# Value products with a head's high and low columns side by side as the stationary operand

## The chip, the cores and the metric

The kernel runs on one core of a Trainium2 chip. The metric is the device time of one execution in microseconds (us), the median of several runs. The core has a matrix engine (TensorE, PE), a vector engine (VectorE, DVE), an activation engine (ScalarE, ACT), a general engine (GpSimd, POOL) and an engine that issues transfers (SyncE, SP). Each works through its own instructions in the order in which they are written; semaphores make one wait for another. Products are summed in PSUM, 2 KB banks that PE writes and ACT and DVE read; everything else on the core lies in SBUF. L581 is line 581 of the kernel.

## The reference, cut to what matters

Two layers of an encoder trunk over 256 positions of width 2048. The change touches the attention; its softmax over three dilated windows comes down, at 256 positions, to one masked softmax for each head.

```python
for l in range(DEPTH):                       # 2
    h = rmsnorm(x, g_pre_mix[l])
    proj = h @ w_in[l]                       # conv | q, k, v of 16 heads x 64 | pooling
    y_a = conformer_conv(...)
    y_b = dilated_attention(proj[..., a_end:b_end], cos, sin)
    y_c = pool_mixer(...)
    y = concatenate([rms_normalize(y_a), rms_normalize(y_b), rms_normalize(y_c)]) * g_mix[l]
    x = x + rmsnorm(y @ w_out[l], g_post_mix[l])
    x = x + rmsnorm(SwiGLU(rmsnorm(x, g_pre_ffn[l])), g_post_ffn[l])
```

In `dilated_attention` each head's output is `o = einsum('bnrhqk,bnkrhe->bnqrhe', p, vwin)` over its 64 value columns, divided by the softmax sum.

## The kernel before

All large products are made in split precision: an operand is kept as a high part (fp32r) and a low part (what is left of the fp32 value), and a product is high x high + high x low + low x high. Weights come in tiles of 128x2x512: SP loads them (raw), ACT writes the high half (L104), DVE the low half (L113), and PE uses them in L139 to L141. Eight such tiles (hl) are in flight. This stream of weight products fills PE all the time; its groups set the steps in which the program is written. The schedule is manual: what is written first stands first on each engine, and the small work of attention is a set of Python generators (tasks) that each write a piece in one step and then give way for one or more steps. So the order of every engine follows from the yields, and no instruction passes another on its engine.

Attention runs in two halves of eight heads (hf 0 and 1), two heads (a pair, pr) after each other. For one head `head_task` writes, in this order: scores on PE (L540, six products, q and k in split form) into the one PSUM buffer sc; mask and row maximum on DVE (L545, two halves, the tile pt); the negated maximum on POOL (L550); exponentials on ACT (L553); normalisation on DVE (L559, L561); four transposes on PE (L568) into a PSUM buffer tr; the high part of the transposed probabilities pT on ACT (L572) and the low part on DVE (L573); the value products on PE (L581) into po. Two heads share one po tile, one PSUM bank, of which there is only one.

The value products have the value columns of both heads of the pair (128 columns) as the stationary operand and 256 columns of pT as the moving one: for each of the two key tiles high v x high pT, high v x low pT, low v x high pT, six in all. Only the half of the output rows that belongs to the head is used (rows 0 to 63 for an even head, 64 to 127 for an odd one). After the odd head ACT writes the high part yB (L597, one instruction for each head's 64 rows, with the gain gT), ACT the squares (L601), and DVE the low part (L603), all reading po; POOL adds the squares up (L608).

The values themselves are made in `v_done`: when a v product of 128 positions by 512 columns is done, ACT writes its high part (L525) and DVE its low part (L526), one instruction each.

The tiles pt, both pT and sq come from one pool, s2, with 6 buffers in rotation: each new tile takes the oldest buffer and must wait for the last reader of what was in it. Other work between these steps: rope on q and k (L486 to L499) and their transposes (L509, L513, L514), the convolution's sums on DVE (L380) and its layer norm (L395 to L412), transposes of the y parts (L206, with ACT L213 and DVE L216, into yTA and yTC), the output of a projection (L679).

Of the kernel before, what the change touches and what calls it, by code (L numbers as in the profile page):

```python
# [7 lines left out]
F32 = mybir.dt.float32  # L8
F32R = mybir.dt.float32r
AF = mybir.ActivationFunctionType  # L10
ALU = mybir.AluOpType
AX = mybir.AxisListType

P = 128
S = 256
NT = S // P
# [6 lines left out]
HD = 64  # L23
ROT = 16
NHH = HALF_B // HD
# [4 lines left out]
NB = 512  # L30
# [11 lines left out]
def hybrid_encoder_kernel(  # L42
# [6 lines left out]
    nc = tc.nc  # L49
# [4 lines left out]
    s4 = ctx.enter_context(tc.tile_pool(name="s4", bufs=23))  # L54
    s2 = ctx.enter_context(tc.tile_pool(name="s2", bufs=6))
# [115 lines left out]
    def tr_free():  # L171

        k = clock["step"]
        if used.get(k):
            return False
        used[k] = True
        return True
# [57 lines left out]
    rs_in = {}  # L235
# [81 lines left out]
    def mixer_jobs(l):  # L317
        st = {}
# [199 lines left out]
        def v_done(hf):  # L518
            def done(t, ps):
                if t == 0:  # L520
                    st["v", hf] = [
                        s4.tile([P, NT, NB], F32R, tag="s4", name="v") for _ in range(2)
                    ]
                hi, lo = (a[:, t] for a in st["v", hf])
                nc.scalar.activation(hi, ps, AF.Copy, scale=rs_in[t])  # L525
                nc.vector.scalar_tensor_tensor(  # L526
                    lo, ps, rs_in[t], hi.bitcast(F32), ALU.mult, ALU.subtract
                )
            return done

        def head_task(hf, h):
            qT, kT, v = st["qT", hf], st["kT", hf], st["v", hf]
            pr, r0 = h // 2, (h % 2) * HD
            sc = scp.tile([P, NT, S], F32, tag="sc", name="sc")
            pt = s2.tile([P, NT, S], F32, tag="s2", name="pt")
            mx = sm.tile([P, NT], F32, tag="mx", name="mx")
            den = sm.tile([P, NT], F32, tag="den", name="den")
            for t in range(NT):
                for i, (a, b) in enumerate(((0, 0), (0, 1), (1, 0))):
                    nc.tensor.matmul(  # L540
                        sc[:, t], qT[a][r0 : r0 + HD, pr, t * P : (t + 1) * P],
                        kT[b][r0 : r0 + HD, pr], start=i == 0, stop=i == 2,
                    )
            for t in range(NT):
                nc.vector.tensor_tensor_reduce(  # L545
                    pt[:, t], sc[:, t], mask[:, (1 - t) * P : (1 - t) * P + S], 1.0, -3.0e38, ALU.add, ALU.max,
                    accum_out=mx[:, t : t + 1],
                )
            nmx = sm.tile([P, NT], F32, tag="nmx", name="nmx")
            nc.gpsimd.tensor_scalar(nmx, mx, -(HD ** -0.5), None, ALU.mult)  # L550
            yield
            for t in range(NT):
                nc.scalar.activation(  # L553
                    pt[:, t], pt[:, t], AF.Exp, bias=nmx[:, t : t + 1], scale=HD ** -0.5,
                    accum_out=den[:, t : t + 1],
                )
            yield
            rden = sm.tile([P, NT], F32, tag="rden", name="rden")
            nc.vector.reciprocal(rden, den)  # L559
            for t in range(NT):  # L560
                nc.vector.tensor_scalar(pt[:, t], pt[:, t], rden[:, t : t + 1], None, ALU.mult)  # L561
            yield 2
            while not tr_free():
                yield
            pst = trp.tile([P, NT, S], F32, tag="tr", name="tr")
            for kt in range(NT):
                for t in range(NT):
                    nc.tensor.transpose(  # L568
                        pst[:, kt, t * P : (t + 1) * P], pt[:, t, kt * P : (kt + 1) * P], ident
                    )  # L570
            pT = [s2.tile([P, NT, S], F32R, tag="s2", name="pT") for _ in range(2)]
            nc.scalar.activation(pT[0], pst, AF.Copy)  # L572
            nc.vector.tensor_tensor(pT[1], pst, pT[0].bitcast(F32), ALU.subtract)  # L573
            yield 2
            if h % 2 == 0:
                st["po", hf] = pop.tile([P, 2, S], F32, tag="po", name="po")
            po = st["po", hf]
            n = 0
            for kt in range(NT):
                for a, b in ((0, 0), (0, 1), (1, 0)):  # L580
                    nc.tensor.matmul(  # L581
                        po[:, h % 2], v[a][:, kt, pr * P : (pr + 1) * P], pT[b][:, kt],
                        start=n == 0, stop=n == 5,
                    )
                    n += 1
            if h % 2 == 0:
                return
            if pr == 0:
                yB[hf] = [s4.tile([P, 4, S], F32R, tag="s4", name="yB") for _ in range(2)]
            hi, lo = yB[hf]  # L590
            col = G_MX + l * KD + 4 + 4 * hf + pr
            sq = sq_acc
            if (hf, pr) != (0, 0):
                sq = s2.tile([P, S], F32, tag="s2", name="sq")
            rows = [slice(e * HD, (e + 1) * HD) for e in range(2)]
            for e, r in enumerate(rows):
                nc.scalar.activation(  # L597
                    hi[r, pr], po[r, e], AF.Copy, scale=gT[r, col : col + 1]
                )
            for e, r in enumerate(rows):  # L600
                nc.scalar.activation(sq[r], po[r, e], AF.Square)  # L601
            for e, r in enumerate(rows):
                nc.vector.scalar_tensor_tensor(  # L603
                    lo[r, pr], po[r, e], gT[r, col : col + 1], hi[r, pr].bitcast(F32),
                    ALU.mult, ALU.subtract,
                )
            if sq is not sq_acc:
                nc.gpsimd.tensor_tensor(sq_acc, sq_acc, sq, ALU.add)  # L608
            if hf == 1 and pr == 3:
                yield 2  # L610
                ssb = scp.tile([P, NT], F32, tag="sc", name="ssb")
                for t in range(NT):
                    nc.tensor.matmul(
                        ssb[:, t : t + 1], sq_acc[:, t * P : (t + 1) * P], ones,
                        start=True, stop=True,
                    )
                ms = sm.tile([P, NT], F32, tag="msb", name="msb")
                nc.vector.tensor_scalar(ms, ssb, 1.0 / C_B, EPS, ALU.mult, ALU.add)
                rs = sm.tile([P, NT], F32, tag="rsb", name="rsb")
                nc.gpsimd.tensor_tensor(  # L620
                    rs, ms, half_neg.to_broadcast([P, NT]), ALU.pow
                )
                for t in range(NT):
                    rs_b[t] = rs[:, t : t + 1]
# [3 lines left out]
        def attn_task(hf, pace):  # L628
            for h in range(NHH):
                spawn(head_task(hf, h))  # L630
                yield pace[h % len(pace)]
# [126 lines left out]
    for l in range(DEPTH):  # L758
        jobs, load_layer = mixer_jobs(l)
        a = len(groups)  # L760
        add_jobs(jobs)
        seg_info.append((a, len(groups), load_layer, (g_post_mix, l), G_FF + l * KD))
        a = len(groups)
# [31 lines left out]
    for n in range(4):  # L795
        for t in range(NT):
            load_x(t, n)
            g = 2 * n + t
# [4 lines left out]
    gT = cst.tile([P, NG], F32, name="gT")  # L803
# [9 lines left out]
    rows = {}  # L813
# [48 lines left out]
    col = None  # L862
    for si, (g0, g1, load_layer, post, pre) in enumerate(seg_info):
        n = g1 - g0
# [98 lines left out]
        col = pre  # L963
# [55 lines left out]
```

## Time and profile before

| | |
|---|---|
| median of 3 runs | 2235.47 us (2235.39 to 2235.93) |
| profiled execution | 2234.84 us, span 2233.0 us |
| PE busy | 2210.7 us, 99% of the span |
| DVE busy | 1287.8 us, 58% |
| ACT busy | 1056.9 us, 47% |
| POOL busy | 136.4 us, 6% |
| chain that ended last | PE 94%, DVE 3%, ACT 2%, issue 1% |
[...]

Attention of layer 1 lies at about 160 to 310 us of the span. How the views below are read: the table by stretch gives for each stretch the busy time of PE, PE's weight loads (PEld), DVE, ACT and POOL with the number of instructions, then the granted clock, the DMA share and GB/s. The list of waits gives an engine's line, what it waited for, the sum in us, how often, and the longest. The groups give line, engine, operation, output<-inputs, shapes and count, then busy us and mean ns of one, then the idle time before them and what ended it. The timeline gives start, duration, engine, line, what is written from what, and how many in a row (x4); in brackets the engine's idle time just before and what ended it. Ends of PE's products are modelled, so starts are compared.

### The profile page before, as it was taken

To read this page: it belongs to the slowest core of one execution; us is meant where nothing else is said; L and a number is where in the kernel's file an instruction comes from. 1 tells how busy PE (TensorE), PEld (TensorE's weight loads), DVE (VectorE), ACT (ScalarE), POOL (GpSimd) and SP (SyncE) were. 2 spreads that over 40 slices of the span, in tenths; PEclk is the share of its full clock that TensorE was granted. 3 is DMA by queue.
4 is the path that set the end of the run, shared out by engine and by line. 5 is a ranking of instruction groups with operands and counts; after the bars stand their busy time and mean duration, and the time that the engine had idled before them with its cause. 6 is when DMAs were issued, how large, how long until landed. Compare 5 with 4: busy or idle time off the path is not lost.

```text
span 2233.0 us, 26297 instructions
## 1 busy us (share of the span) xinstructions
PE 2210.7 (99%) x9858; PEld 1781.1 (80%) x9858; DVE 1287.8 (58%) x1735; ACT 1056.9 (47%) x1465; POOL 136.4 (6%) x179
## 2 busy tenths in 40 slices
PE   9999999999999999999999999999999999999998
PEld 7888887888888888888778788878888888888886
DVE  5798757445444544445567987565444444444544
ACT  6445756444444443444554566564444444434442
POOL 0001113000000000000210011120000000000002
PEclk9999999999999999999999999999999999999999
DMA  7654355555556555556565544555555555555553
GB/s 264 197 174 137 133 173 171 184 180 187 187 182 187 184 184 187 187 182 199 177 201 177 171 131 150 171 162 187 180 186 186 186 186 180 187 186 183 188 198 122
DMA packets 208608, 400.66 MB, mean 179 GB/s; under 512 B 12730, under 2 KB 16162, under 8 KB 208480
## 3 DMA queue, kind: packets, MB, share of 16 engines
q1 hardware_dynamic: 208448, 398.98, 55.3%
q8 instruction: 77, 1.26, 0.2%
q14 instruction: 51, 0.42, 0.1%
q10 hardware_dynamic: 32, 0.01, 0.0%
HBM read 396.84 MB, written 2.10 MB: 179 GB/s over the span
## 4 chain that ended last, share of the span: by engine, by line
PE 94%; DVE 3%; ACT 2%; issue 1%; DMA 0%; POOL 0%; SPq 0%; DVEq 0%; POOLq 0%; ACTq 0%
PE acc L139 30%; PE acc L140 30%; PE acc L141 30%; PE tr L206 1%; PE sc L540 1%; PE po L581 1%; DVE hl L113 1%; PE tr L568 1%; ACT xT L213 0%; DVE x L290 0%; DVE xT L216 0%; ACT hl L104 0%; ACT junk L200 0%; PE tr L509 0%; PE tr L442 0%
## 5 line engine op out<-in xcount | busy, mean ns | idle before, releaser
L113 DVE TENSOR_TENSOR hl<-raw,hl 128x1024 fp32r<-128x1024 f32 x736 | 905.2, 1231 | 769.3 <-ACT hl L104 767.8
L104 ACT ACTIVATE hl<-raw 128x1024 fp32r<-128x1024 f32 x735 | 776.6, 1059 | 762.7 <-PE acc L141 752.7
L139 PE MATMUL acc<-hl,xT 128*128 128x512 f32 x1984 | 797.0, 402 | 0.0
L140 PE MATMUL acc<-hl,xT 128*128 128x512 f32 x1984 | 787.7, 397 | 0.6 <-DVE hl L113 0.5
L141 PE MATMUL acc<-hl,xT 128*128 128x512 f32 x1984 | 787.4, 397 | 0.0
L141 PEld LDWEIGHTS acc<-hl,xT 128*128 128x128 f32 x1984 | 374.4, 189 | 90.8
L140 PEld LDWEIGHTS acc<-hl,xT 128*128 128x128 f32 x1984 | 374.5, 189 | 88.6 <-DVE hl L113 2.2
L139 PEld LDWEIGHTS acc<-hl,xT 128*128 128x128 f32 x1984 | 374.4, 189 | 88.6
L139 PE MATMUL acc<-hl,fT 128*128 128x512 f32 x704 | 280.1, 398 | 0.0
L141 PE MATMUL acc<-hl,fT 128*128 128x512 f32 x704 | 279.1, 396 | 0.0
L140 PE MATMUL acc<-hl,fT 128*128 128x512 f32 x704 | 279.0, 396 | 0.0
L141 PEld LDWEIGHTS acc<-hl,fT 128*128 128x128 f32 x704 | 132.6, 188 | 32.3
L140 PEld LDWEIGHTS acc<-hl,fT 128*128 128x128 f32 x704 | 132.7, 188 | 31.7
L139 PEld LDWEIGHTS acc<-hl,fT 128*128 128x128 f32 x704 | 132.6, 188 | 31.8
L270 POOL TENSOR_TENSOR out<-out,gain 128x512 f32<-128x512 f32 x20 | 25.8, 1300 | 1448.2 <-ACT junk L200 1448.2
L380 DVE SCALAR_TENSOR_TENSOR cacc<-hT,cwT,cacc 128x241 f32<-128x241 f32 (+14 forms) x240 | 98.7, 469 | 0.0
L208 ACT ACTIVATE fT<-tr 128x512 fp32r<-128x512 f32 x44 | 26.4, 599 | 96.1 <-PE tr L206 96.1
L209 DVE TENSOR_TENSOR fT<-tr,fT 128x512 fp32r<-128x512 f32 x44 | 30.4, 692 | 68.6 <-ACT fT L208 68.6
L200 ACT ACTIVATE junk<-out 128x512 bf16<-128x512 f32 x32 | 20.2, 631 | 68.3 <-DVE out L737 43.4
L707 ACT ACTIVATE sg<-acc,rsin 128x512 f32<-128x512 f32 x44 | 30.4, 691 | 45.6 <-PE acc L141 45.6
L139 PE MATMUL acc<-hl,yB 128*128 128x512 f32 x128 | 51.1, 399 | 0.0
L140 PE MATMUL acc<-hl,yB 128*128 128x512 f32 x128 | 50.7, 396 | 0.0
(150 smaller groups left out, 1299.2 us busy)
## 6 DMA issues: line engine op xcount, KB each, us to landing
raw<-in_w_gate_dram SPq DMA_DIRECT2D x176, 512.0 KB, 3.5
raw<-in_w_up_dram SPq DMA_DIRECT2D x176, 512.0 KB, 3.5
raw<-in_w_down_dram SPq DMA_DIRECT2D x176, 512.0 KB, 3.6
raw<-in_w_in_dram SPq DMA_DIRECT2D x144, 512.0 KB, 3.6
raw<-in_w_out_dram SPq DMA_DIRECT2D x64, 512.0 KB, 3.6
x<-in_x_dram SPq DMA_DIRECT2D x8, 256.0 KB, 6.9
pm<-in_c_pool_dram SPq DMA_DIRECT2D x4, 512.0 KB, 5.2
gain<-in_g_post_mix_dram SPq DMA_DIRECT2D x4, 512.0 KB, 6.6
```

Of the source, the lines that this page charges most:

```text
L104: nc.scalar.activation(hl[:, 0], raw, AF.Copy)
L113: nc.vector.tensor_tensor(hl[:, 1], raw, hl[:, 0].bitcast(F32), ALU.subtract)
L139: nc.tensor.matmul(ps, xh, hl[:, 0, j], start=first, stop=False)
L140: nc.tensor.matmul(ps, xh, hl[:, 1, j], start=False, stop=False)
L141: nc.tensor.matmul(ps, xl, hl[:, 0, j], start=False, stop=last)
L206: nc.tensor.transpose(pst[:, j], srcs[j], ident)
L208: nc.scalar.activation(dst[:, 0], pst, AF.Copy)
L209: nc.vector.tensor_tensor(dst[:, 1], pst, dst[:, 0].bitcast(F32), ALU.subtract)
L270: nc.gpsimd.tensor_tensor(o, o, gain, ALU.mult)
L380: nc.vector.scalar_tensor_tensor(acc[:, c, lo:hi], src, w, acc[:, c, lo:hi], ALU.mult, ALU.add)
L540: nc.tensor.matmul(sc[:, t], qT[a][r0 : r0 + HD, pr, t * P : (t + 1) * P], kT[b][r0 : r0 + HD, pr], start=i == 0, stop=i == 2,)
L707: nc.scalar.activation(sg[t], ps, AF.Silu, scale=rs_in[t])
```

## The change

The value tile of one key tile is now laid out as 8 heads x 2 x 64: an even head's high columns come first and its low columns behind them, an odd head's low columns first. So 128 columns of one head are the stationary operand, and one product gives high v x pT in 64 output rows and low v x pT in the other 64. With pT's high and low parts and two key tiles that is four products a head. Then the two halves of rows are added: ACT copies the low half from po into the other half's rows of a new tile yv (L594), and DVE adds the two into yv (L595), for each head. After the odd head hi, square and lo read yv, 128 rows at a time (L606, L607, L608). The tile yv is one more tile of the pool s2 for each pair of heads. In `v_done` each 128x512 instruction becomes two of 128x4x64, for the even and the odd heads (L528, L529). Lines behind move by 3 to 5: L540 to L543, L545 to L548, L550 to L553, L553 to L556, L559 and L561 to L562 and L564, L568 to L571, L572 and L573 to L575 and L576, L581 to L585.

```diff
@@ v_done
-                        s4.tile([P, NT, NB], F32R, tag="s4", name="v") for _ in range(2)
+                        s4.tile([P, NHH, 2, HD], F32R, tag="s4", name="v") for _ in range(NT)
                     ]
-                hi, lo = (a[:, t] for a in st["v", hf])
-                nc.scalar.activation(hi, ps, AF.Copy, scale=rs_in[t])
-                nc.vector.scalar_tensor_tensor(
-                    lo, ps, rs_in[t], hi.bitcast(F32), ALU.mult, ALU.subtract
-                )
+                v = st["v", hf][t].rearrange("p (g e) c d -> p g e c d", e=2)
+                pv = ps.rearrange("p (g e d) -> p g e d", e=2, d=HD)
+                for e in range(2):
+                    hi, lo = v[:, :, e, e], v[:, :, e, 1 - e]
+                    nc.scalar.activation(hi, pv[:, :, e], AF.Copy, scale=rs_in[t])
+                    nc.vector.scalar_tensor_tensor(
+                        lo, pv[:, :, e], rs_in[t], hi.bitcast(F32), ALU.mult, ALU.subtract
+                    )
@@ head_task
             for kt in range(NT):
-                for a, b in ((0, 0), (0, 1), (1, 0)):
+                vv = v[kt][:, h].rearrange("p c d -> p (c d)")
+                for b in range(2):
                     nc.tensor.matmul(
-                        po[:, h % 2], v[a][:, kt, pr * P : (pr + 1) * P], pT[b][:, kt],
-                        start=n == 0, stop=n == 5,
+                        po[:, h % 2], vv, pT[b][:, kt], start=n == 0, stop=n == 3,
                     )
                     n += 1
+            e = h % 2
+            r, r2 = slice(e * HD, (e + 1) * HD), slice((1 - e) * HD, (2 - e) * HD)
+            if e == 0:
+                st["yv", hf] = s2.tile([P, 2, S], F32, tag="s2", name="yv")
+            yv = st["yv", hf]
+            nc.scalar.activation(yv[r, 1], po[r2, e], AF.Copy)
+            nc.vector.tensor_tensor(yv[r, 0], po[r, e], yv[r, 1], ALU.add)
             if h % 2 == 0:
                 return
...
-            rows = [slice(e * HD, (e + 1) * HD) for e in range(2)]
-            for e, r in enumerate(rows):
-                nc.scalar.activation(
-                    hi[r, pr], po[r, e], AF.Copy, scale=gT[r, col : col + 1]
-                )
-            for e, r in enumerate(rows):
-                nc.scalar.activation(sq[r], po[r, e], AF.Square)
-            for e, r in enumerate(rows):
-                nc.vector.scalar_tensor_tensor(
-                    lo[r, pr], po[r, e], gT[r, col : col + 1], hi[r, pr].bitcast(F32),
-                    ALU.mult, ALU.subtract,
-                )
+            y, g = yv[:, 0], gT[:, col : col + 1]
+            nc.scalar.activation(hi[:, pr], y, AF.Copy, scale=g)
+            nc.scalar.activation(sq, y, AF.Square)
+            nc.vector.scalar_tensor_tensor(
+                lo[:, pr], y, g, hi[:, pr].bitcast(F32), ALU.mult, ALU.subtract
+            )
```

The order of PE's other products, of POOL and of SP is the same. Below, at the first pair of heads of layer 1 (heads 0 and 1, their products done at about 200 us), is what stands in a row on DVE before; pt_1763 is head 3's score tile, po_1652 the pair's output, hl tiles are weights, yA the convolution's branch.

```order
L561 TENSOR_SCALAR pt_1671<-pt_1671,rden_1758 128x256
L545 ISA pt_1763,mx_1764<-sc_1762,mask_134 128x256 [waits PE_49,Pool_49]
L545 ISA mx_1764 128x1
L545 ISA pt_1763,mx_1764<-sc_1762,mask_134 128x256
L545 ISA mx_1764 128x1
L113 TENSOR_TENSOR hl_1778<-raw_1635,hl_1778 128x1024 [waits DMAHW7_49,Activation_49]
L404 TENSOR_SCALAR yA_1632<-tr_1707,mv_1743,rstd_1747 128x512 [waits Pool_49]
L408 TENSOR_TENSOR yA_1632<-yA_1632,lnp_826 128x512 [waits DVE_49]
L409 TENSOR_TENSOR yA_1632<-yA_1632,lnp_826 128x512 [waits DVE_49]
L603 SCALAR_TENSOR_TENSOR yB_1803<-po_1652,gT_132,yB_1802 64x256 [waits PE_49,Activation_49]
L603 SCALAR_TENSOR_TENSOR yB_1803<-po_1652,gT_132,yB_1802 64x256
L113 TENSOR_TENSOR hl_1814<-raw_1684,hl_1814 128x1024 [waits DMAHW0_49,Activation_49]
```

The same place on DVE after the change; pt_1768 is head 3's score tile, yv_1661 the first pair's new tile and yv_1836 the second pair's.

```order
L564 TENSOR_SCALAR pt_1676<-pt_1676,rden_1763 128x256
L548 ISA pt_1768,mx_1769<-sc_1767,mask_134 128x256 [waits PE_49,Pool_49]
L548 ISA mx_1769 128x1
L548 ISA pt_1768,mx_1769<-sc_1767,mask_134 128x256
L548 ISA mx_1769 128x1
L113 TENSOR_TENSOR hl_1783<-raw_1639,hl_1783 128x1024 [waits DMAHW7_49,Activation_49]
L404 TENSOR_SCALAR yA_1636<-tr_1712,mv_1748,rstd_1752 128x512 [waits Pool_49]
L408 TENSOR_TENSOR yA_1636<-yA_1636,lnp_826 128x512 [waits DVE_49]
L409 TENSOR_TENSOR yA_1636<-yA_1636,lnp_826 128x512 [waits DVE_49]
L595 TENSOR_TENSOR yv_1661<-po_1656,yv_1661 64x256 [waits Activation_49]
L608 SCALAR_TENSOR_TENSOR yB_1808<-yv_1661,gT_132,yB_1807 128x256 [waits Activation_49]
L113 TENSOR_TENSOR hl_1816<-raw_1689,hl_1816 128x1024 [waits DMAHW0_49,Activation_49]
```

The addition stands where the first low part stood. Head 3's L548 waits for PE as L545 did, but the product it waits for is another: before, head 3's own scores; now also head 1's value products, the last readers of the buffer that the tile takes over.

On ACT before, at the same place:

```order
L104 ACTIVATE hl_1778<-raw_1635 128x1024 [waits DMAHW7_49]
L597 ACTIVATE yB_1802<-po_1652,gT_132 64x256 [waits PE_49]
L597 ACTIVATE yB_1802<-po_1652,gT_132 64x256
L601 ACTIVATE sq_acc_103<-po_1652 64x256 x2
L553 ACTIVATE pt_1763,den_1765<-pt_1763,nmx_1774 128x256 [waits Pool_49]
L553 ACTIVATE pt_1763,den_1765<-pt_1763,nmx_1774 128x256 [waits DVE_49]
L104 ACTIVATE hl_1814<-raw_1684 128x1024 [waits DMAHW0_49]
```

And on ACT after:

```order
L104 ACTIVATE hl_1783<-raw_1639 128x1024 [waits DMAHW7_49]
L594 ACTIVATE yv_1661<-po_1656 64x256 [waits PE_49]
L606 ACTIVATE yB_1807<-yv_1661,gT_132 128x256 [waits DVE_49]
L607 ACTIVATE sq_acc_103<-yv_1661 128x256
L556 ACTIVATE pt_1768,den_1770<-pt_1768,nmx_1779 128x256 [waits Activation_49,Pool_49]
L556 ACTIVATE pt_1768,den_1770<-pt_1768,nmx_1779 128x256
L104 ACTIVATE hl_1816<-raw_1689 128x1024 [waits DMAHW0_49]
L594 ACTIVATE yv_1836<-po_1831 64x256 [waits PE_49]
```

Between the pair's products and the exponentials ACT now waits twice, for PE and then for DVE's addition. The v tiles on ACT after the change, first half of the heads, show the third place (the conversions of the first and of the second 128 positions):

```order
L528 ACTIVATE v_1338<-acc0_1167,rsin0_405 128x4x64 [waits PE_49]
L528 ACTIVATE v_1338<-acc0_1167,rsin0_405 128x4x64 [waits DVE_49]
L104 ACTIVATE hl_1356<-raw_1279 128x1024 [waits DMAHW2_49,PE_49,Activation_49]
L104 ACTIVATE hl_1377<-raw_1300 128x1024 [waits DMAHW3_49,PE_49,Activation_49]
L104 ACTIVATE hl_1398<-raw_1327 128x1024 [waits DMAHW4_49,PE_49,Activation_49]
L104 ACTIVATE hl_1418<-raw_1354 128x1024 [waits DMAHW5_49,PE_49,Activation_49]
L528 ACTIVATE v_1339<-acc1_1269,rsin1_443 128x4x64 [waits PE_49]
L528 ACTIVATE v_1339<-acc1_1269,rsin1_443 128x4x64 [waits DVE_49]
```

Each second half waits for DVE's first half, where before one instruction stood that waited for PE alone.

## Rows read from the trace of the kernel before

**Rows 1.** Table by stretch of the span, three stretches of layer 1's attention.

```profile
150.00:186.00 36.00, 36.00 (x162) 28.48 (x161) 35.23 (x78) 16.72 (x24) 2.85 (x3) 1.00 0.56 176
...
223.00:240.00 17.00, 17.00 (x94) 14.42 (x93) 14.07 (x30) 16.30 (x34) 3.52 (x6) 1.00 0.38 133
...
260.00:300.00 40.00, 39.86 (x209) 33.07 (x209) 26.26 (x62) 26.42 (x57) 5.95 (x9) 1.00 0.47 157
```

**Rows 2.** List of PE's waits, whole span: the value products' own.

```profile
PE po L581 <- DVE yB L603: 0.8, 2, 0.4
```

**Rows 3.** Timeline of PE: head 0's value products and what follows them.

```profile
186.45 0.88 PE L581 MATMUL po<-pT,v 128*128 128x256 f32 x6
187.17 0.60 PE L509 MATMUL tr<-ident,q 128*128 128x128 f32 x4
```

**Rows 4.** Groups of instructions: those that the change replaces.

```profile
L603 DVE SCALAR_TENSOR_TENSOR yB<-po,gT,yB 64x256 fp32r<-64x256 f32 x32 | 15.4, 483 | 29.0 <-ACT sq L601 28.8
L597 ACT ACTIVATE yB<-po,gT 64x256 fp32r<-64x256 f32 x32 | 15.0, 470 | 26.5 <-PE po L581 26.1
...
L601 ACT ACTIVATE sq<-po 64x256 f32<-64x256 f32 x28 | 10.6, 379 | 0.3
L526 DVE SCALAR_TENSOR_TENSOR v<-acc,rsin,v 128x512 fp32r<-128x512 f32 x8 | 6.0, 744 | 3.9 <-ACT v L525 3.9
```

**Rows 5.** Timeline: a score pass on DVE, and PE's scores that need it.

```profile
184.91 0.42 DVE L545 CUSTOM_DVE_ANT_0 pt<-sc,mask 128x256 f32<-128x256 f32 x1
...
187.70 0.73 PE L540 MATMUL sc<-kT,qT 64*128 64x256 f32 x4
```

**Rows 6.** Timeline of DVE around the first pair's low parts.

```profile
198.47 0.42 DVE L545 CUSTOM_DVE_ANT_0 pt<-sc,mask 128x256 f32<-128x256 f32 x1
...
202.47 0.97 DVE L603 SCALAR_TENSOR_TENSOR yB<-po,gT,yB 64x256 fp32r<-64x256 f32 x2
204.27 1.23 DVE L113 TENSOR_TENSOR hl<-raw,hl 128x1024 fp32r<-128x1024 f32 x1 [0.83 <-ACT hl L104]
```

**Rows 7.** Timeline of ACT in the same stretch.

```profile
200.43 0.96 ACT L597 ACTIVATE yB<-po,gT 64x256 fp32r<-64x256 f32 x2 [3.00 <-PE po L581]
...
202.20 0.51 ACT L553 ACTIVATE pt<-pt,nmx 128x256 f32<-128x256 f32 x1
...
203.20 1.04 ACT L104 ACTIVATE hl<-raw 128x1024 fp32r<-128x1024 f32 x1
```

**Rows 8.** Timeline of PE: head 2's products, and the second transposes of yC.

```profile
203.59 0.95 PE L581 MATMUL po<-pT,v 128*128 128x256 f32 x6 [0.40 <-DVE yB L603]
...
212.41 0.60 PE L206 MATMUL tr<-ident,yC 128*128 128x128 f32 x4
```

**Rows 9.** Timeline of DVE: low parts of yC's transposes, and the next weights.

```profile
210.98 1.12 DVE L216 SCALAR_TENSOR_TENSOR yTC<-tr,gT,yTC 128x128 fp32r<-128x128 f32 x4 [1.18 <-ACT yTC L213]
...
212.90 1.23 DVE L113 TENSOR_TENSOR hl<-raw,hl 128x1024 fp32r<-128x1024 f32 x1 [0.80 <-ACT hl L104]
```

**Rows 10.** Timeline of ACT around the second pair's high parts.

```profile
226.28 0.94 ACT L597 ACTIVATE yB<-po,gT 64x256 fp32r<-64x256 f32 x2
...
230.95 1.04 ACT L104 ACTIVATE hl<-raw 128x1024 fp32r<-128x1024 f32 x1
```

**Rows 11.** Timeline of DVE in the same stretch.

```profile
228.89 0.97 DVE L603 SCALAR_TENSOR_TENSOR yB<-po,gT,yB 64x256 fp32r<-64x256 f32 x2
...
233.16 1.12 DVE L216 SCALAR_TENSOR_TENSOR yTA<-tr,gT,yTA 128x128 fp32r<-128x128 f32 x4
```

**Rows 12.** Timeline of PE: transposes of k, and later scores of the second half.

```profile
235.48 0.49 PE L509 MATMUL tr<-ident,k 128*128 128x128 f32 x3
...
247.52 0.50 PE L540 MATMUL sc<-kT,qT 64*128 64x256 f32 x2
```

**Rows 13.** Timeline of ACT and DVE ahead of those scores.

```profile
242.12 1.06 ACT L104 ACTIVATE hl<-raw 128x1024 fp32r<-128x1024 f32 x1
...
245.41 0.42 DVE L545 CUSTOM_DVE_ANT_0 pt<-sc,mask 128x256 f32<-128x256 f32 x1
```

## The prediction

> **What bounds the kernel now.** I read the table by stretch first [rows 1]: TensorE (PE) is busy all of the time in 150 to 186 and in 223 to 240 us, and all but 0.14 us in 260 to 300 us. So the time falls only if PE is given less to do, and rises with every new wait of PE. Then PE's waits over the whole span: at the value products, line L581, it waits for VectorE (DVE) twice, 0.4 us each, once in either layer [rows 2]. The other engines run just ahead of it, and the same table shows how close: in 150 to 186 us DVE is busy 35.23 of 36 us, in 223 to 240 us ScalarE (ACT) 16.30 of 17 us; only from 260 us on, where the second eight heads run, are both busy two thirds of the time. So PE is the bound, with thin cover in the first half of each layer's attention. The question is not what the removed products are worth, but whether DVE and ACT keep ahead of PE where the change lengthens their chain. All places below are in layer 1; the same sequence comes again in layer 2, so each counts twice.
>
> **What is removed from PE.** Six products of one head take 187.17 - 186.45 = 0.72 us from their first start to the next line's start, 0.12 us each [rows 3]. Two fewer for each of 32 heads: 64 x 0.12 = 7.7 us, 0.24 us a head, 3.84 us a layer. The products keep their shape (128 x 128 stationary, 256 columns). If nothing else moved, the time would be 2235.47 - 7.7 = 2227.8 us.
>
> **Prices of the new work.** Even and odd heads each get a copy of 64x256 on ACT: 0.38 us, as the square of the same shape from the same place [rows 4]. Each gets an addition of 64x256 on DVE; the nearest rows are the score pass, 128x256 from PSUM, 0.42 us [rows 6], and L603, the same shape with one multiplication more, 0.48 us [rows 4]; I take 0.42. The odd head's four ACT instructions and two DVE instructions of 64 partitions become hi, square and lo on 128 partitions with the same 256 columns, for which I take the same times, 0.47, 0.38 and 0.48 [rows 4]. In sum little changes: for a pair of heads ACT had 1.70 us and gets 1.61, DVE had 0.97 and gets 1.32.
>
> What counts is that they now form a chain with two more hand-overs: products, ACT copy, DVE addition, ACT hi, DVE lo. Before, ACT took hi straight from the products; now ACT, which works in its written order, stands still after its copy until DVE has come to the addition, and all that is queued behind it on ACT (the next head's exponentials L553, the high halves of weights L104, and so DVE's low halves L113) waits too.
>
> [...]
>
> **The v tiles.** Each 128x512 conversion on ACT and on DVE becomes two of 128x4x64, and they alternate: ACT, DVE, ACT, DVE, each waiting for the one before. At 256 columns DVE has 0.48, some 0.5 of waiting for ACT's second half (0.47), and 0.48, against 0.74 before [rows 4]: 0.7 us more a tile. In the first eight heads this falls into DVE's full stretch, two tiles, 1.4 us. The cover there is 2.4 us: the second half of a score pass that starts at 184.91 ends at 185.33, and PE's L540 that needs it starts at 187.70 [rows 5]. So no stall; the cover shrinks to about 1.0.
>
> **Place (a), head 2's products at 203.59.** The s2 pool has 6 buffers, and the change takes one more for each pair of heads (yv). By the order of allocation head 3's score tile now falls on the buffer that head 1's products read (the high half of its transposed probabilities), so DVE's L548 (L545 before) must wait for these products. Before, it starts at 198.47 [rows 6]; the products are done at 200.43, where they release ACT's L597 [rows 7]; less the 0.48 saved by then, 199.95. That is 1.5 us later. Behind it on DVE stand L113, L404, L408 and L409, and then the addition in L603's place, 4.0 us of work from 198.47 to 202.47 [rows 6]. The addition starts at 203.97, ends at 204.39, and PE follows 0.15 us later (as 203.59 follows 202.47 + 0.97) [rows 6, 8]: 204.54. PE would have come at 203.59 - 0.48. Added wait 1.4 us; PE is now 0.95 us later than before, after head 2 0.7.
>
> **Place (b), L206 at 212.41.** ACT's hi starts at 204.45 instead of 200.43, its exponentials at 205.3 instead of 202.20, the high halves at 206.3 instead of 203.20 [rows 7]. DVE's low halves, released by them at 204.27 [rows 6], come at 207.4. From 204.27 DVE had work without a gap until 210.98 - 1.18 = 209.80 [rows 9]; with head 2's addition that is 5.9 us: 213.3, then four L216 of 1.12 us in all, 214.4, PE at 214.5. PE would come at 212.41 + 0.7 [rows 8]. Added wait 1.4; PE 2.1 later, after heads 3 and 4 1.6.
>
> **Place (c), L509 at 235.48.** DVE is 2.3 us late at the end of L216 and regains the 0.80 us in which it waited before the next L113 [rows 9]: 1.5 late. The addition, in L603's place at 228.89 [rows 11], then ends at 230.8, and ACT has waited for it since 228.2. Hi and square take 0.85; behind them ACT has 2.9 us of work up to L104 (226.28 + 1.70 to 230.95) [rows 4, 10]: L104 at 234.6, 3.7 us late. L216 ends 3.3 us behind it (233.16 + 1.12 against 230.95) [rows 10, 11]: 237.9; PE at 238.1 instead of 235.48 + 1.6 [rows 12]. Added wait 1.0; PE 2.6 later, after head 5 2.4.
>
> **Place (d), L540 at 247.52.** ACT is full up to here (0.7 us idle in 17) [rows 1] and can regain that much. It carries 3.7 us late; head 4's copy adds 0.4; the first v tile of the second eight heads takes it 2.2 instead of 0.7, since its second half waits for a DVE that has three L113 ahead of it; head 5's copy, some 1.2 of waiting for the addition, hi and square make 2.4 against 1.7. 3.7 + 0.4 + 1.5 + 0.7 - 0.6 = 5.7: L104 at 247.8 instead of 242.12. The score pass that PE waits for ends 3.7 us behind it (245.41 + 0.42 against 242.12) [rows 13]: 251.5; PE at 251.65 instead of 247.52 + 2.4 [rows 12]. Added wait 1.7. From here ACT and DVE have a third of their time free [rows 1]; the other ten heads' products I take as gain alone.
>
> **Sum.** Waits 1.4 + 1.4 + 1.0 + 1.7 = 5.5 us a layer against 3.84 saved: +1.7, in two layers +3.4. On the profiled execution, 2234.84 us (span 2233.0), that is 2238.2; on the median, 2235.47 and 0.03% above it, 2238.9. POOL, SP and the transfers keep their order. If the new instructions are each 0.1 us off, a place moves by 0.3 to 0.4, since three or four of them stand in its chain: 1.6 a layer, 3.2 in all, 2235.7 to 2242.1.
>
> **Rivals.** *The covers hold (faster).* PE alone decides: 2227.8 us, up to 2231 if one place keeps a small wait. For it: PE waits at L581 for 0.8 us in all today. It decides at (a) and (b): the odd head's addition has to end by 202.9, and L216 by 211.6. Against it: with the buffer wait the first is 1.5 us late. *No buffer wait.* Were head 3's tile free in time, the addition would end at 202.9 and (a) would cost nothing; ACT is still held 2.5 us for it, so (b) to (d) stay: 4.1 - 3.84 = +0.3 a layer, 2236. *The v halves break DVE's full stretch (slower).* In 150 to 186 us DVE has 0.8 us to spare. If a tile costs it 1.5 us rather than 0.7, as when a hand-over queues behind a weight conversion of ACT (L104, 1.04 us [rows 7]), the two tiles take 3.0 of 2.4 us of cover: PE waits 0.6 there, and the later places start with nothing in hand, some 0.6 more at three of them. That is 2.4 a layer more, 2243.7, and up to 2248 if lateness runs on into the second eight heads. It decides from 1.2 us a tile.
>
> **How the numbers follow.** A measurement of this kernel tells about 0.2% (4.5 us: 2231.0 to 2239.9) from no change. The forecast has 0.45 (0.28 of it below 2239.9, 0.17 above), the covers 0.20, no buffer wait 0.15, the v halves 0.20. Faster 0.20, same 0.28 + 0.15 = 0.43, slower 0.17 + 0.20 = 0.37. The range leaves out most of the covers' case and the end of the v case: 2230.5 to 2245.
>
> **What would show it.** In the profile after, PE's waits should list the value products (L585) and L206, L509 and the scores (L543) behind DVE, 1 to 2 us each, twice each; the idle time of ACT before hi (L606) should be led by DVE's addition (L595); PE's work should shrink by 7.7 us while the span does not. If PE's waits stay near 1 us, the walk is wrong from (a) on and the time is near 2228. If PE waits before 186 us, the v halves are the cause.

## The result, and the profile after

The change makes the kernel slower: median 2247.39 us (2245.14 to 2248.01, 4 runs) against 2235.46 us, ratio 1.0052, 95% interval 1.0039 to 1.0066. That is 11.9 us, where 3.4 us slower was forecast, and 2.4 us beyond the upper end of the range, 2245. The profiled execution took 2248.01 us (span 2246.2), the longest of the four; the one before 2234.84. The 13.2 us between these two are taken apart here.

PE does what it was given: 128 value products instead of 192, at the same pitch (head 0's four start at 186.83 us and the next line at 187.31, 0.12 us each), and each head's 0.24 us are to be seen all through attention. The list of PE's waits over the span, which for these lines held only [rows 2] before, now reads (sum in us, times, longest):

```profile
PE sc L543 <- DVE mx L548: 6.1, 4, 2.1
...
PE po L585 <- DVE yv L595: 3.7, 2, 1.8
...
PE tr L206 <- DVE yTC L216: 1.6, 2, 0.8
...
PE tr L571 <- DVE pT L576: 1.2, 2, 0.6
PE tr L571 <- DVE qT L514: 1.0, 2, 0.5
...
PE tr L509 <- DVE yTA L216: 0.8, 2, 0.4
```

These are 14.4 us against 0.8, each of them in both layers. Every place that the prediction named is in it, and two that it did not name, both at L571. 13.6 us more waiting less the 7.7 us saved would be 6 us; most of the rest, as the last table of this section shows, is TensorE's clock, granted at 0.995 over the profiled run against 0.997 before. The table by stretch of the changed kernel (busy us and number of instructions of PE, PEld, DVE, ACT, POOL, then granted clock, DMA share, GB/s):

```profile
250.00:254.00 4.00, 1.90 (x11) 1.48 (x10) 3.35 (x7) 2.49 (x4) 1.11 (x2) 0.90 0.23 76
254.00:259.00 5.00, 5.00 (x15) 3.91 (x15) 2.98 (x7) 2.04 (x5) 0.68 (x2) 0.50 0.44 154
...
1369.00:1373.00 4.00, 4.00 (x14) 3.11 (x13) 3.10 (x7) 2.04 (x5) 0.95 (x2) 0.57 0.60 218
```

Behind the wait of 2.1 us at L543 the granted clock is 0.50 for more than 5 us, and PE gets through 15 instructions where the kernel before got through 27 in the same five microseconds:

```profile
254.00:259.00 5.00, 5.00 (x27) 4.09 (x26) 2.16 (x6) 3.69 (x7) 0.74 (x1) 1.00 0.38 128
```

The groups of the new instructions answer to [rows 4] (busy us, mean ns of one, idle time of the engine before them and what ended it):

```profile
L548 DVE CUSTOM_DVE_ANT_0 pt<-sc,mask 128x256 f32<-128x256 f32 x64 | 24.4, 418 | 2.3 <-PE po L585 2.2
...
L595 DVE TENSOR_TENSOR yv<-po,yv 64x256 f32<-64x256 f32 x32 | 13.4, 420 | 17.0 <-ACT yv L594 16.7
...
L594 ACT ACTIVATE yv<-po 64x256 f32<-64x256 f32 x32 | 12.1, 379 | 30.9 <-PE po L585 30.6
...
L606 ACT ACTIVATE yB<-yv,gT 128x256 fp32r<-128x256 f32 x16 | 8.2, 510 | 20.4 <-DVE yv L595 20.4
L608 DVE SCALAR_TENSOR_TENSOR yB<-yv,gT,yB 128x256 fp32r<-128x256 f32 x16 | 7.8, 485 | 9.2 <-ACT yB L606 9.2
L529 DVE SCALAR_TENSOR_TENSOR v<-acc,rsin,v 128x256 fp32r<-128x256 f32 x16 | 7.7, 481 | 4.3 <-ACT v L528 4.3
...
L528 ACT ACTIVATE v<-acc,rsin 128x256 fp32r<-128x256 f32 x16 | 7.6, 472 | 21.0 <-DVE v L529 17.6 <-PE acc L141 3.4
...
L607 ACT ACTIVATE sq<-yv 128x256 f32<-128x256 f32 x14 | 5.6, 402 | 0.0
```

The prices were right: copy 379 ns (0.38 us taken), addition 420 (0.42), lo 485 (0.48), v halves 472 and 481 (0.47, 0.48). Only hi and the square are a little dearer, 510 ns against 0.47 us and 402 against 0.38. ACT stands 20.4 us before hi, all of it for DVE's addition, and 17.6 us before second halves of v.

Since the weight products L139 to L141 are the same and in the same order in both kernels, the difference of their start times in the two traces shows where time is lost. It rises or falls at few places (us; layer 2 repeats layer 1 but for the clock; waits with the 0.24 of a head that fall into the same step added back):

```
place in the kernel after            forecast   layer 1   layer 2
L571 at 192.75 (head 1)                 0         0.72      0.72
L571 at 196.81 (head 2)                 0         0.81      0.82
(a) L585, head 2                        1.4       1.47      1.47
(b) L206, second yC                     1.4       1.02      1.04
(c) L509                                1.0       0.63      0.64
(d) L543, 253.30                        1.7       2.1       2.1
L543 at 269.31                          0         0.83      0.84
sum of waits                            5.5       7.6       7.6
lower clock after (d)                   0         3.0       1.5
saved, 16 heads                        -3.8      -3.8      -3.8
layer                                  +1.7      +6.8      +5.3
```

Another 0.8 us net is lost behind 366 us: in this execution of the changed kernel the granted clock is 0.66 over 372 to 377 us, where the kernel before has 1.00 in 366 to 372. It stands behind a wait of PE of 2.6 us at L206 that both kernels have (364.98 in the kernel before), and no run shows that the change brought it about. The rest is rounding and the start of the program.

### The profile page after: what moved, and what is told of

Same layout as the page of the kernel before. It is cut to its first block, busy times and chain, and to the rows that moved or that the text cites. A ratio compares the mean times of both kernels' runs of the same rounds, so it can differ in the third digit from the quotient of the medians.

```text
span 2246.2 us, 26187 instructions
## 1 busy us (share of the span) xinstructions
PE 2210.7 (98%) x9794; PEld 1777.8 (79%) x9794; DVE 1294.3 (58%) x1759; ACT 1052.6 (47%) x1473; POOL 136.6 (6%) x179
## 4 chain that ended last, share of the span: by engine, by line
PE 90%; DVE 5%; ACT 3%; issue 1%; POOL 1%; DMA 0%; SPq 0%; POOLq 0%; DVEq 0%; ACTq 0%
PE acc L139 29%; PE acc L140 29%; PE acc L141 29%; DVE hl L113 2%; PE tr L206 1%; PE sc L543 1%; ACT hl L104 1%; ACT pt L556 1%; PE po L585 0%; DVE xT L216 0%; DVE x L290 0%; DVE pt L548 0%; ACT xT L213 0%; PE tr L571 0%; ACT junk L200 0%
## 5 line engine op out<-in xcount | busy, mean ns | idle before, releaser
L113 DVE TENSOR_TENSOR hl<-raw,hl 128x1024 fp32r<-128x1024 f32 x736 | 905.6, 1232 | 777.0 <-ACT hl L104 776.1
L139 PE MATMUL acc<-hl,xT 128*128 128x512 f32 x1984 | 798.4, 402 | 0.0
L141 PE MATMUL acc<-hl,xT 128*128 128x512 f32 x1984 | 787.7, 397 | 0.0
L141 PEld LDWEIGHTS acc<-hl,xT 128*128 128x128 f32 x1984 | 375.0, 189 | 91.1
L139 PEld LDWEIGHTS acc<-hl,xT 128*128 128x128 f32 x1984 | 375.0, 189 | 88.8
L139 PE MATMUL acc<-hl,fT 128*128 128x512 f32 x704 | 280.1, 398 | 0.0
L141 PE MATMUL acc<-hl,fT 128*128 128x512 f32 x704 | 279.1, 396 | 0.0
L141 PEld LDWEIGHTS acc<-hl,fT 128*128 128x128 f32 x704 | 132.6, 188 | 32.3
L139 PEld LDWEIGHTS acc<-hl,fT 128*128 128x128 f32 x704 | 132.6, 188 | 31.8
L139 PE MATMUL acc<-hl,yB 128*128 128x512 f32 x128 | 51.1, 399 | 0.0
```

The lines of the kernel that those rows point to most:

```text
L113: nc.vector.tensor_tensor(hl[:, 1], raw, hl[:, 0].bitcast(F32), ALU.subtract)
L139: nc.tensor.matmul(ps, xh, hl[:, 0, j], start=first, stop=False)
L141: nc.tensor.matmul(ps, xl, hl[:, 0, j], start=False, stop=last)
```

## The experiments

Each ratio is to the kernel before as measured with that run: 2234.90 us for the runs up to the first with a later hi, 2234.74 for the last three, 2235.46 with the change. So a difference in us to the change is uncertain by some 0.7 us.

**The v tiles alone, taken out.** Every head has its high columns first, so a v conversion is one instruction of 128x8x64 again. Copy and addition stay as they are for odd heads too, since the sum of the two halves of rows does not depend on which of them holds the high columns.

```diff
-                v = st["v", hf][t].rearrange("p (g e) c d -> p g e c d", e=2)
-                pv = ps.rearrange("p (g e d) -> p g e d", e=2, d=HD)
-                for e in range(2):
-                    hi, lo = v[:, :, e, e], v[:, :, e, 1 - e]
...
+                v = st["v", hf][t]
+                pv = ps.rearrange("p (h d) -> p h d", d=HD)
+                hi, lo = v[:, :, 0], v[:, :, 1]
...
```

> The changed kernel, but every head has its high columns first, so that each v conversion is again one instruction of 128x8x64 on ACT and one on DVE (no alternation). Theory A (the v halves make DVE 1.5 us late in its full stretch, 150 to 186 us, and the lateness lasts, since DVE's later waits there are for ACT, which waits for DVE): the two new waits of PE at L571 near 192.7 and 196.8 us (together 1.1 us a layer in the list of waits, 1.5 in the distance to the kernel before) go, and of the waits at the scores (6.1 us in all) those that the second half's v halves feed shrink; 3 to 4 us a layer, 2237 to 2241 us, less if the clock stays at its upper level. Theory B (the recorded prediction: the cover absorbs the first two tiles): only the second half's v tiles count, under 2 us a layer, 2243 to 2246 us.

Measured: 2237.52 us, ratio to the kernel before 1.0012 (1.0003 to 1.0022), 9.9 us less than the change. PE's waits in attention:

```profile
PE po L584 <- DVE yv L594: 3.7, 2, 1.8
...
PE sc L542 <- DVE mx L547: 1.9, 4, 0.7
PE tr L509 <- DVE yTA L216: 1.5, 2, 0.8
```

Both waits at L571 are gone, and the scores' waits fall from 6.1 to 1.9 us. So theory A holds: DVE's lateness from the first half's v tiles does last, and the second half's feed (d). The list shows 7.3 us of waits fewer (8.0 by the starts of the weight products). Most of what is left of the 9.9 us is the clock: it no longer falls behind (d) (1.00 over 250 to 258 us), though it now falls behind (a) (0.66 over 206 to 211).

**The v halves alone, put into the kernel before** (old layout, six products).

```diff
...
+                vh, vl = (
+                    a[:, t].rearrange("p (g e d) -> p g e d", e=2, d=HD) for a in st["v", hf]
+                )
+                pv = ps.rearrange("p (g e d) -> p g e d", e=2, d=HD)
+                for e in range(2):
+                    hi, lo = vh[:, :, e], vl[:, :, e]
+                    nc.scalar.activation(hi, pv[:, :, e], AF.Copy, scale=rs_in[t])
+                    nc.vector.scalar_tensor_tensor(
+                        lo, pv[:, :, e], rs_in[t], hi.bitcast(F32), ALU.mult, ALU.subtract
+                    )
```

> The kernel before, with each v conversion cut into two of 128x4x64 on ACT and DVE as in the change (old layout, six products). Theory A: DVE is 1.5 us late from 168 us on, the least distance of a DVE result to PE's need after it is 0.65 to 1.5 us (at 191.9 and 195.2), so PE waits 1 us or more a layer there and again at 260 us: 2238 to 2240 us. Theory B (cover 2.4 us holds in the first half): 2235.5 to 2237 us.

Measured: 2239.39 us, ratio 1.0021 (1.0011 to 1.0030): theory A. PE's waits:

```profile
PE po L586 <- DVE yB L608: 1.8, 2, 0.9
PE sc L545 <- DVE mx L550: 1.6, 2, 0.8
...
PE tr L573 <- DVE pT L578: 1.2, 2, 0.6
```

4.6 us against 0.8, and no lower clock in attention of layer 1 (1.00 in the stretches 204 to 212 and 254 to 262 us). The halves cost 4 to 5 us by themselves. Of the two places at L571 only the second (196.81) is in this list; at the first, 192.75, the starts grow by 0.15 us against 0.72 with the whole change.

**The buffer alone, held in the kernel before.** From each even head to its odd head one more s2 buffer is held, by a tile of which POOL writes one column and copies it to another.

```diff
             if h % 2 == 0:
+                st["held", hf] = s2.tile([P, 2, S], F32, tag="s2", name="held")
+                nc.gpsimd.memset(st["held", hf][:, 0, :1], 0.0)
                 return
...
+            held = st["held", hf]
+            nc.gpsimd.tensor_scalar(held[:, 0, 1:2], held[:, 0, :1], 1.0, None, ALU.mult)
```

> The kernel before, with one more s2 buffer held from each even head to its odd head (a tile of which POOL writes and reads one column; nothing else is changed). Theory A (place (a) is the buffer wait): L545 of the head that takes over the buffer starts when head 1's products are done, about 200.4 instead of 198.5 us, L603 and with it PE's products of head 2 come 1.5 to 2 us later, in both layers: 2238 to 2240 us, and PE's wait at L581 grows from 0.8 to 4 to 5 us. If the wait is hidden: within 1 us of the kernel before.

Measured: 2244.32 us, ratio 1.0042 (1.0026 to 1.0058), 4 us beyond what theory A expected. The wait is as expected; timelines of DVE and PE at place (a):

```profile
200.69 0.43 DVE L545 CUSTOM_DVE_ANT_0 pt<-sc,mask 128x256 f32<-128x256 f32 x1 [1.88 <-PE po L581]
...
204.69 0.98 DVE L605 SCALAR_TENSOR_TENSOR yB<-po,gT,yB 64x256 fp32r<-64x256 f32 x2
```

```profile
205.82 1.62 PE L581 MATMUL po<-pT,v 128*128 128x256 f32 x6 [2.36 <-DVE yB L605]
```

L545 starts 2.2 us later than [rows 6], L605 (L603 before) likewise, and PE's wait grows from 0.40 [rows 8] to 2.36, in the sum of both layers from 0.8 to 4.7: 3.9 us. The other 5.5 us stand behind it, in the table by stretch:

```profile
203.00:206.00 3.00, 0.64 (x3) 0.23 (x3) 2.89 (x6) 1.76 (x5) 0.00 (x0) 0.91 0.55 175
206.00:212.00 6.00, 6.00 (x21) 5.06 (x22) 3.93 (x10) 1.54 (x2) 0.86 (x1) 0.50 0.28 87
```

After the wait the granted clock is at 0.50 for more than 6 us. Between the weight products on both sides of this place the difference to the kernel before grows by 4.74 us, 2.0 of waiting and 2.75 of the lower clock, and by 4.95 in layer 2. So 2 us of added waiting cost more than twice that.

**hi, square and lo one step later**, with straight v tiles. ACT has its next exponentials and weights ahead of hi.

```diff
             y, g = yv[:, 0], gT[:, col : col + 1]
+            last = hf == 1 and pr == 3
+            if not last:
+                yield
             nc.scalar.activation(hi[:, pr], y, AF.Copy, scale=g)
```

> As the run with straight v tiles, and the odd head's hi, square and lo are written one step later than its addition (except for the last pair), so that ACT does not stand before DVE's addition with the next exponentials and weights behind it. If ACT's standing wait is what places (b), (c) and (d) cost, some 3 us a layer more go: 2229 to 2235 us. If the buffer wait alone starts the chain, the time stays within 1.5 us of the run without the later hi.

Measured: 2234.85 us, ratio 1.0000 (0.9991 to 1.0010), 2.7 us less than with straight v tiles alone, just inside what the first theory expected. Of PE's waits in attention one line is left:

```profile
PE po L584 <- DVE yv L594: 3.7, 2, 1.8
```

(c) and the scores are gone from the list ((b) was so already with straight v tiles), and ACT's hi waits 2.7 us in all for the addition instead of 21.9. That alone does not prove that they came from ACT's standing before hi, since PE also comes later to these places, by the lower clock; the last two runs below show it without a fall of the clock. But (a) is whole, and behind it the clock falls for longer than in the run before:

```profile
206.00:211.00 5.00, 5.00 (x15) 3.83 (x14) 3.79 (x11) 1.69 (x3) 1.05 (x1) 0.50 0.34 105
```

Here the whole gain of 7.7 us goes into one place: 2.9 us of added waiting in both layers, and by the same comparison of starts some 6 us at the lower clock in the profiled execution (2236.65 us, 1.8 above the median). The ten executions differ by the clock as well: the six with a mean granted clock of 0.994 have a median of 2236.65 us, the four with 0.996 one of 2233.77.

**yv taken late.** Nothing is done after an even head; after the odd head's products yv is taken and both copies and both additions read po. The tile of the next head is then never short of a buffer.

```diff
...
             if h % 2 == 0:
                 return
...
+            rows = [slice(e * HD, (e + 1) * HD) for e in range(2)]
+            yv = s2.tile([P, 2, S], F32, tag="s2", name="yv")
+            for e in range(2):
+                nc.scalar.activation(yv[rows[e], 1], po[rows[1 - e], e], AF.Copy)
+            for e in range(2):
+                nc.vector.tensor_tensor(
+                    yv[rows[e], 0], po[rows[e], e], yv[rows[e], 1], ALU.add
+                )
```

With the v halves of the change:

> The changed kernel with its v halves, but the tile yv is taken only after the odd head's products (both copies and both additions then, from po), so that no score tile waits for a buffer that value products still read. Theory A (the buffer wait makes place (a) and helps to start the fall of the clock): the added 1.47 us at (a) go in both layers, DVE's wait for PE at L548 (2.2 us in the groups) goes, the waits at 192.7 and 196.8 us stay; 3 to 6 us less than the changed kernel, 2241 to 2244 us. If DVE's lateness from the v tiles alone makes PE wait at (a): no more than 1 us less, above 2246 us.

Measured: 2243.08 us, ratio 1.0035 (1.0022 to 1.0049), 4.3 us less than the change: theory A. DVE's wait for the products before L548 is gone, and PE's wait at L585 falls from 3.7 to 2.1 us (longest 1.0): by the starts 0.64 us a layer is left at (a) of 1.47, so not all of it was the buffer wait. The scores' wait stays (6.6 us, longest 1.9); the granted clock over the profiled run was 0.996. With straight v tiles:

> Straight v tiles and the late yv, hi still right behind the additions. What is left is ACT's standing wait for DVE's additions, places (b) to (d). Theory A (three separate causes that add up): place (a) costs 0.3 to 0.5 us against 0.48 saved, (c) and (d) about 0.5 to 1 us each; 2229 to 2232 us, with PE's waits in attention under 4 us. Rival (ACT's wait alone carries the loss, whatever starts it): 2234 us and more, as in the run with the later hi.

Measured: 2233.02 us, ratio 0.9991 (0.9982 to 1.0000), 1 us above the expected range and within 0.2% of the kernel before. The waits are small and spread:

```profile
PE sc L542 <- DVE mx L547: 2.2, 4, 0.6
PE tr L509 <- DVE yTA L216: 1.4, 2, 0.7
PE po L584 <- DVE yv L597: 1.4, 2, 0.7
...
PE tr L206 <- DVE yTC L216: 0.9, 2, 0.4
```

These are 5.9 us, where under 4 were expected, and 5.1 beyond the 0.8 of before. No wait is longer than 0.7 us, and the granted clock is 1.00 in the stretches 196 to 220 and 246 to 270 us, where the change (0.50 over 254 to 259), the held buffer (0.50 over 206 to 212) and the two versions with straight v tiles and the early yv (0.50 over 208 to 210) have their falls.

**All three: straight v tiles, yv late, hi a step later.**

> Straight v tiles, late yv, and hi, square and lo one step later. Theory A: PE's waits in attention fall to about those of the kernel before (0.8 us at the value products), so the 7.7 us of removed products remain whole: 2227.5 to 2229.5 us. Rival (the longer chain copy, addition, hi costs PE time somewhere in any order): 2231 us and more.

Measured: 2227.51 us (2227.07 to 2228.28, 6 runs), ratio 0.9966 (0.9954 to 0.9978): 7.2 us faster than the kernel before and faster than every other version here. PE's waits in attention are

```profile
PE po L584 <- DVE yv L597: 1.5, 2, 0.7
```

against 0.8, and the differences of the starts fall by 0.24 us at every head but head 2, where L584 waits, in both layers. ACT's hi waits 3.3 us in all instead of 20.4 in the change and 22.0 in the run before this one:

```profile
L609 ACT ACTIVATE yB<-yv,gT 128x256 fp32r<-128x256 f32 x16 | 8.0, 503 | 3.3 <-DVE yv L597 3.2
```

Only hi's place differs between these two runs, and the clock is 1.00 in attention of layer 1 in both. So the 4.4 us of waits that go from one to the other, among them those of (b), (c) and the scores, were ACT's standing before hi. The four products were worth what the first sum said, 7.7 us less 0.7 at L584; nothing else in the new chain shows as a wait of PE in this order.

## Why the prediction was right or wrong

Right: the mechanism and its sign against the clean gain. The saving is 0.24 us a head. The buffer wait exists (DVE idle 2.2 us in all before L548, released by the value products), it delays the addition behind L113, L404, L408 and L409, and place (a) cost 1.47 us where 1.4 was worked out. ACT stands before hi for the addition, and (b) and (c) follow from it: with straight v tiles and late yv the later hi takes both away. Of the rivals, the held buffer and the late yv rule out the one without a buffer wait, and 14.4 us of waits the one in which the covers hold. The 2227.8 us of that one were met only with straight v tiles, late yv and a later hi (2227.51). One name was wrong: the tile that takes over the buffer (pt_1768) is head 4's, not head 3's; the wait and its place are the same.

Wrong, the step "So no stall; the cover shrinks to about 1.0". DVE was late by 1.5 us, about the 1.4 worked out (the score pass that PE needs at 187.7 started at 186.79 in the kernel after instead of 184.91, of which 0.4 is the whole program's shift). But the cover was read at one place. The next ones are thinner. For the second of the two places at L571, DVE's and PE's rows of the kernel before:

```profile
193.86 0.68 DVE L573 TENSOR_TENSOR pT<-tr,pT 128x512 fp32r<-128x512 f32 x1
```

```profile
195.18 0.49 PE L568 MATMUL tr<-ident,pt 128*128 128x128 f32 x3
```

Here 0.64 us lie between the end of the one and the start of the other. DVE does not recover on the way, because the idle time in front of its next weights (1.42 us before and after) is a wait for ACT, which waits through POOL for DVE's own score pass. DVE before, then after:

```profile
188.65 1.22 DVE L113 TENSOR_TENSOR hl<-raw,hl 128x1024 fp32r<-128x1024 f32 x1 [1.42 <-ACT hl L104]
```

```profile
190.54 1.23 DVE L113 TENSOR_TENSOR hl<-raw,hl 128x1024 fp32r<-128x1024 f32 x1 [1.42 <-ACT hl L104]
```

The rows at the second place after:

```profile
196.07 0.68 DVE L576 TENSOR_TENSOR pT<-tr,pT 128x512 fp32r<-128x512 f32 x1
```

```profile
196.81 0.66 PE L571 MATMUL tr<-ident,pt 128*128 128x128 f32 x4 [0.59 <-DVE pT L576]
```

That is 1.5 us a layer at the two places. At the first, 192.75, the cover was 1.47 us (DVE's L514 ended at 190.47, PE came at 191.94), and the halves alone only just used it up; the rest of the 0.72 is head 0's addition, which stands on DVE just ahead of L514 (0.34 us), and the 0.24 us by which PE came earlier. The rival on the v halves had this chain right (later places start with nothing in hand) and its point of decision wrong: no dearer tile was needed, 0.7 us was enough.

Wrong in size: (b) 1.02 and (c) 0.63 against 1.4 and 1.0, since PE came there later than forecast, mostly by the two early waits, and by more than DVE did (1.9 us against 1.6 at (b), 1.6 against 1.3 at (c)); (d) 2.1 against 1.7; and the scores at 269.31, 16 us behind it, which I took as covered, 0.83. The sum of waits is 7.6 a layer against 5.5: 4.2 us of the miss in two layers.

Missing altogether: the clock. Every term was priced at the granted clock of 1.00 that all of these stretches showed. But that was the clock of a PE that waited 0.4 us at most in these stretches. Behind the 2.1 us at (d) it fell to 0.50 in both layers, which cost 3.0 and 1.5 us; with the 0.8 behind 366 us, which may not be the change's, that is 5.3 us, the larger part of the miss. 3.4 + 4.2 + 5.3 = 12.9 of the 13.2 us.

Hi and the square, for which the times of before were taken, came out 40 ns (510 against 470) and 23 ns (402 against 379) dearer. Their shape (64x256 to 128x256) and their source (po to yv) changed together, and no run tells which of the two it was. At the three places where they stand in ACT's chain, (b) to (d), that is an estimated 0.4 us in both layers.

The three causes do not simply add. Straight v tiles gave 9.9 us with the early yv and 10.1 with the late one; late yv gave 4.3, 4.5 and, once hi was later, 7.3; later hi gave 2.7 with the early yv and 5.5 with the late one. In the two runs with straight v tiles and the early yv, one large wait left over, at (a), has the lower clock behind it, and that hides what the others gained.

What stays open: which waits bring the clock down. In the kernel after, 1.8 us at (a) left it at 1.00 in 204 to 223 us, while 1.8 us at (a) took it to 0.50 in the runs with straight v tiles. Nothing run here tells these apart. The kernel before had shown as much: the same wait of PE stands in both layers, and only in layer 2 does the clock fall behind it.

```profile
364.98 0.66 PE L206 MATMUL tr<-ident,x 128*128 128x128 f32 x4 [2.60 <-DVE xT L216]
...
1472.54 0.66 PE L206 MATMUL tr<-ident,x 128*128 128x128 f32 x4 [2.60 <-DVE xT L216]
```

```profile
366.00:372.00 6.00, 5.57 (x27) 4.27 (x26) 5.14 (x8) 4.80 (x15) 3.55 (x3) 1.00 0.47 145
...
1473.00:1477.00 4.00, 4.00 (x13) 3.14 (x12) 3.78 (x9) 4.00 (x11) 1.29 (x2) 0.57 0.26 76
```

So a lower clock behind such a wait could have been a term of the sum, with a chance rather than a fixed price. Nor was the later hi tried on the change with nothing else, or the v halves with both other causes gone.

## What to carry to other kernels

Where one engine is the bound and the others run just ahead of it, a change that takes work from it is decided by the distances between each of its operands and its need, all along the stretch behind the edit, not at the nearest one (here 2.4 us at the nearest, 1.47 and 0.64 us at the two places at L571); lateness of an engine lasts as long as its idle time is a wait in a loop that leads back to itself (DVE's 1.42 us before and after). Here an added hand-over cost next to nothing (0.7 us) once what waits was written behind the work that is ready, and an added tile once it was taken late: the same four products were 0.5% slower or 0.3% faster by the order, the time at which the tile is taken and the layout of v. A wait of TensorE of 2 us is to be priced with the lower clock that came behind some of them here, 1.5 to 3 us a place.

## What the runs showed of the hardware

After waits of TensorE of 1.8 to 2.6 us the granted clock was 0.50 for 3 to 7 us (0.57 over 1473 to 1477 us behind L206 in the kernel before, 0.50 over 206 to 212 behind (a) with the held buffer), and the time lost to it in attention, 1.5 to 3 us a place, was about as large as the wait (2.36 us of waiting and 2.75 us of clock with the held buffer). Not every wait of that length was followed by it: 1.8 us at (a) in the kernel after was not, nor 2.60 us at L206 in layer 1 of the kernel before.

A strided conversion of 128x8x64 into every other 64 columns took 688 ns on ACT and 749 ns on DVE in the fastest version (686 and 745 with straight v tiles and the late yv), against 685 and 744 for the contiguous 128x512 in the kernel before: here the layout itself costs no more than 5 ns.
